# Parts of W_out spread over 46 steps of attention instead of 50, with the heads' parts and turned blocks placed anew, and another order at the boundary to the MLP

## The chip, the cores and the metric

The kernel runs on one core of a Trainium2 chip. The metric is the device time of one execution in microseconds (us), as the median of several runs. A core has five engines that run side by side, each with its own queue of instructions: TensorE (PE, matmuls and transposes), VectorE (DVE), ScalarE (ACT), GpSimd (POOL) and SyncE (SP), whose queue issues the DMAs. They wait for one another through semaphores.

## The reference, cut to what matters

One layer of a trunk with four token mixers side by side, on x of 1024 positions by 1024 columns; then an MLP of width 4096; then a final norm. The mixer that matters here is A, attention with 4 heads and two softmax maps per head.

```python
def _diff_attention(q, k, v, lam, lam_init, subln_g):
    ...
        s = jnp.einsum('bqhmd,bkhmd->bhmqk', q_blk, k,
                       preferred_element_type=jnp.float32) * scale + bias[None, :, None]
        p = jax.nn.softmax(s, axis=-1)
        w = p[:, :, 0] - lam * p[:, :, 1]
        return jnp.einsum('bhqk,bkhe->bqhe', w.astype(v.dtype), v)
...
        y = jnp.concatenate([y_a, y_b, y_c, y_d], axis=-1)
        x = x + y @ w_out[l]
        xn2 = _rmsnorm(x, norm2_g[l])
        x = x + jnp.square(jax.nn.relu(xn2 @ w_up[l])) @ w_down[l]
    return _rmsnorm(x, final_g)
```

## The kernel before

Rows of x (positions) are handled in 8 row blocks of 128, called tb. A product in float32 is made of three matmuls (`mm3`) of values split into a high and a low part; a split is a cast on ACT (L110) and a subtraction on DVE or POOL (L111). The MLP's product with w_up is made of products of sums of blocks, which is why normed rows are added to one another and turned (transposed) in several combinations: B11, B21, B22 and T1 to T4.

**Attention** (`attention`, L737) runs 64 steps x = 4n + kp, four for each of 16 pairs of a head and two query blocks. In a step PE does in turn: the scores of step x + 6, into a "big" bank (DVE takes the maximum, L648, ACT the exponential, L655, and for a step's pair of maps the two are combined on POOL, on ACT and POOL, or on DVE, L673); `turned`, four transposes of the weights into an "sm" bank (taken out by ACT, L688, or DVE, L690); some of the `fillers`; the step's late items; and `apply` of the step before, 8 matmuls into the "av" bank. There are three "sm" banks, two "big" and one "av".

**Fillers** are the 64 parts of W_out for the mixers B, C and D, spread evenly over the first SL steps (`self.fill`), with a DVE add for every second (L801).

**Late items** come from the table `LATE`. `w_out_a(pr)` gives a list for the row blocks 2pr and 2pr + 1: item 0 is `attended` (4 transposes of the heads' result, taken out by ACT, L767, and DVE, L768); items 1 to 4 are `rows(i, j)`, six matmuls and a DVE add (L833) for a half of a row block. After a row block's second half its sum goes out to `xs` and is normed: ACT squares (L210), DVE scales (L128), POOL takes the power (L124), DVE multiplies (L212). Items 5 to 8 of the pairs 0 and 1 are turns, B11 and B21, two each. A turn is four transposes, two from each of the pair's two normed row blocks, taken out by an ACT cast (L110) and DVE (L111). The lists a0, a1, a2 are those of the pairs 0, 1 and 2. The turns of pair 2, and all of pair 3, are left for the boundary.

**The boundary** (`mlp`, L1157) mixes four kinds of work: f1[p] and f2[p], the first and second half of the first product of w_up's pair p, 12 matmuls each; t, pair 2's ten remaining turns, t[0] and t[1] being B22 and t[2] to t[9] T1 to T4; a, pair 3's items, `attended`, four rows, and ten turns that alternate between the "sm" and "av" banks; and loads and sums of w_up's blocks: `up_load(0)` starts two DMAs (L914), `up_sums(0)` makes four sums on DVE (L919 to L922). After t[1] two sums each of L852 and L853 are made.

**What sets the order.** PE's instructions keep the order of the program (`mm` and `tr` ask for it). For the other engines a scheduler sets the order within each queue before the run. A tile name such as T17 is a buffer: a new tile of that name waits until the last reader of the old one is done.

Of the kernel before, what the change touches and what calls it, by code (L numbers as in the profile page):

```python
# [28 lines left out]
LAM_INIT = 0.8 - 0.6 * math.exp(-0.3 * 0)  # L29
HALF = math.sqrt(0.5)  # L30
NVEC = 77
SL = 50
AHEAD = 6


def LATE(a0, a1, a2):

    return {50: a0[:2], 51: a0[2:3], 52: a0[3:4], 53: a0[4:5] + a1[:1], 54: a1[1:2], 55: a1[2:3],
            56: a1[3:4] + a0[5:7], 57: a1[4:5] + a0[7:8], 58: a0[8:], 59: a2[:1], 60: a2[1:2] + a1[5:6],
            61: a2[2:3] + a1[6:7], 62: a2[3:4] + a1[7:8], 63: a2[4:5] + a1[8:]}, a2[5:]  # L40

# [3 lines left out]
class Trunk:  # L47
# [680 lines left out]
    def attention(self):  # L728
        N = 4 * HEADS
        ahead = 6  # L730
        a = {pr: self.w_out_a(pr) for pr in range(4)}
        late, rest = LATE(a[0], a[1], a[2])
        for n in range(N):
            for kp in range(4):
                m, step = divmod(4 * n + kp + ahead, 4)
                if m < N:
                    self.scores(m, step)  # L737
                self.turned(n, kp)
                if n > 0:
                    if kp == 1:  # L740
                        self.heads_out(n - 1)
                    if kp == 2:
                        self.heads_scaled(n - 1)
                x = 4 * n + kp
                if x < SL:
                    self.fill(64 * (x + 1) // SL - 64 * x // SL)
                for f in late.get(x, ()):
                    f()
                if x == 58:
                    self.first_load(0)  # L750
                if x == 60:
                    self.first_weights(0)
                if kp > 0:
                    self.apply(n, kp - 1)
            self.apply(n, 3)
        self.turns2 = rest
        self.tail = a[3]
# [402 lines left out]
    def mlp(self):  # L1160
        self.heads_out(15)
        self.heads_scaled(15)
        self.fill(len(self.fillers))
        a, t = self.tail, self.turns2
        f1, f2 = zip(*(self.first_parts(p) for p in range(AHEAD)))
        run = lambda fs: [f() for f in fs]
        self.first_load(1)
        self.first_weights(1)
        self.first_load(2)
        run([f1[0], t[0], f1[1], a[0], f2[0], t[1], a[1], a[2], f2[1]] + t[2:4] + a[3:5] + [f1[2]] + t[4:6] + [f1[3]]  # L1170
            + t[6:8] + [f2[2]] + t[8:10] + a[5:7] + [f2[3]])
        self.up_load(0)
        run(a[7:9] + [f1[4]] + a[9:11] + [f1[5]] + a[11:13])
        self.up_sums(0)
        self.split_s12(0)
        run([f2[4]] + a[13:] + [f2[5]])
        self.split_s34(0)
        self.split_a22(0)
        self.again(0)
        self.again(1)  # L1180
        self.up_load(1)
        for p in range(DFF // P // 2):
            self.up_pair(p)
        self.down()
# [25 lines left out]
    def run(self):  # L1210
        self.constants()
        self.groups = [6, 3, 4, 7, 5, 0, 1, 2]
        for x in range(2 * TAPS):
            self.at(16 + 5 * x // 8, lambda x=x: self.conv_tap(x // TAPS, x % TAPS))
        self.at(26, self.mixer_d_load, self.mixer_c_load, self.bias_rows, self.lam)
        for g in range(4):
            self.at(43 + g, lambda g=g: self.mixer_d_gate(g))
        for x in range(4):
            self.at(48 + x, lambda x=x: self.mixer_d_out(x // 2, x % 2))
        for q in range(4):  # L1220
            self.at(42 + q, lambda q=q: self.mixer_c_channels(q))
        self.at(47, self.mixer_c_eight)
        for x in range(4):
            self.at(53 + x, lambda x=x: self.mixer_c_positions(x // 2, x % 2))
        self.at(50, self.mixer_b_load)
        for x in range(4):
            self.at(57 + x, lambda x=x: self.mixer_c_out(x // 2, x % 2))
        for q in range(4):
            self.at(56 + q, lambda q=q: self.mixer_b_norm(q))
        for x in range(4):  # L1230
            self.at(60 + x, lambda x=x: self.mixer_b_silu(x % 2, x // 2))
        for x in range(2):
            self.at(62 + x, lambda x=x: self.scores(0, x))

        self.phase_x()
        self.mixer_b_cols()
        self.mixer_d_v()
        self.mixer_c_cols()
        self.qk_cols(0)
        self.qk_cols(1)  # L1240
        self.st, self.ks, self.qt, self.yt = {}, {}, {}, {}
        self.p1 = ["T14", "gain", "X8", "X9", "X10", "X11"]
        self.subln_s = self.t("sublns", [P, 1])
        self.nc.vector.tensor_scalar(self.subln_s, self.subln, 1.0 - LAM_INIT, None, op0=ALU.mult)
        self.v_cols()
        assert not self.side
        self.wring = ["W0", "W1", "W2", "W3", "W6", "W7"]
        self.load_v()
        self.ya = [self.t(("X14", "X15")[i], [P, 4, 256]) for i in range(2)]
        for x in range(4):  # L1250
            self.scores(*divmod(2 + x, 4))
            self.mixer_b_out(x // 2, x % 2)
        self.fillers += self.w_out_bcd()
        self.ua, self.ub, self.us, self.raw, self.sc, self.xo, self.xn1, self.first_raw = ({} for _ in range(8))
        self.attention()
        self.mlp()
# [99 lines left out]
```

## Time and profile before

| What | Value |
|---|---|
| median of 3 runs | 1133.89 us |
| lowest, highest | 1133.78, 1135.02 us |
| profiled execution | 1133.86 us |
| its span in the profile | 1131.7 us |
| its mean granted clock of TensorE | 0.991 of full speed |
| busy: PE, DVE, ACT, POOL | 96%, 65%, 44%, 27% of the span |

The span is the profile's stretch from the first to the last instruction; 2.2 us of the execution lie around it. Attention runs from about 245 to 473 us of the span, the boundary from there to about 526 us, and the rest of the MLP after it. A wait is shown in the rows as the idle time before an instruction with the instruction that released it, as in `[2.35 <-DVE X L111]`. Busy shares are averages over stages that are bound by different things; a stage is read by itself.

### The profile page before, as it was taken

Reading aid. Unit: us, or ns where it says so; the run is one execution under the profiler, and the core shown is the slowest. Engines: PE = TensorE matmul, PEld = TensorE weight load, DVE = VectorE, ACT = ScalarE, POOL = GpSimd, SP = SyncE. Lnnn points to the kernel's source line nnn. Section 1 sums busy time; section 2 is a strip of 40 time slices with the busy share of each in tenths; the row PEclk is TensorE's granted clock in tenths of the full one; section 3 lists DMA queues with packets and bytes.
Section 4 is the critical chain, followed back from the end, with each engine's and each line's share of the span. In section 5 each row is a group of like instructions: output and inputs, shape, how many; then the busy total and the mean of one; then the engine's idle time right before and its main releaser. Section 6 shows DMA issues by size and latency. Waiting matters only on the chain.

```text
span 1131.7 us, 15023 instructions
## 1 busy us (share of the span) xinstructions
PE 1085.0 (96%) x5836; PEld 918.4 (81%) x5836; DVE 736.6 (65%) x928; ACT 500.7 (44%) x787; POOL 310.5 (27%) x256
## 2 busy tenths in 40 slices
PE   4999999989999998999999999999999999999997
PEld 4989887878999997878777888888778888777885
DVE  4549989758777679785454444434785555986665
ACT  5411313275566656464344444545343333333442
POOL 2000000125456572102777454553400000000001
PEclk9999999999999999999999999999999999999999
DMA  7213126674122102266564444445975553224203
GB/s 270 63 41 92 38 67 212 168 222 157 45 66 71 52 1 94 94 219 228 175 207 177 167 140 168 140 152 162 402 267 171 193 191 117 94 94 168 93 19 149
DMA packets 56660, 159.63 MB, mean 141 GB/s; under 512 B 6411, under 2 KB 8715, under 8 KB 56589
## 3 DMA queue, kind: packets, MB, share of 16 engines
q1 hardware_dynamic: 55581, 156.18, 41.5%
q0 software_dynamic: 1008, 2.49, 0.7%
q8 instruction: 46, 0.75, 0.3%
q14 instruction: 25, 0.20, 0.1%
HBM read 110.41 MB, written 49.28 MB: 141 GB/s over the span
## 4 chain that ended last, share of the span: by engine, by line
PE 84%; DVE 7%; ACT 3%; DMA 2%; issue 2%; SPq 0%; POOL 0%; DVEq 0%; POOLq 0%; ACTq 0%
PE big L104 38%; PE sm L104 32%; PE av L104 10%; PE sm L107 3%; DVE W L111 2%; ACT W L110 1%; DVE T L111 1%; DVE c L648 1%; DMA gain<-in_norm_g_dram 1%; PE av L107 1%; DMA stg<-in_w_out_dram 1%; DVE T L212 0%; DVE T L393 0%; ACT T L210 0%; DVE T L1075 0%
## 5 line engine op out<-in xcount | busy, mean ns | idle before, releaser
L104 PE MATMUL big<-X,W 128*128 128x512 f32 x864 | 211.9, 399 | 2.4 <-DVE T L1007 2.4
L110 ACT CAST W<-stg 128x1024 fp32r<-128x1024 f32 (+1 forms) x93 | 92.1, 994 | 247.9 <-PE big L104 152.8
L104 PEld LDWEIGHTS big<-X,W 128*128 128x128 f32 x864 | 162.9, 190 | 42.1 <-DVE T L1007 4.6
L111 DVE TENSOR_TENSOR W<-stg,W 128x1024 fp32r<-128x1024 f32 x78 | 100.0, 1283 | 128.1 <-ACT W L110 128.0
L124 POOL TENSOR_TENSOR c<-c,mhalf 128x1 f32<-128x1 f32 (+3 forms) x46 | 35.8, 778 | 477.3 <-DVE c L128 405.7
L104 PE MATMUL big<-T,W 128*128 128x512 f32 x648 | 158.7, 397 | 1.1 <-DVE T L111 1.1
L104 PEld LDWEIGHTS big<-T,W 128*128 128x128 f32 x648 | 122.2, 189 | 29.8 <-DVE T L111 1.5
L648 DVE TENSOR_REDUCE c<-big 128x1 f32<-128x1024 f32 x64 | 77.7, 1217 | 26.1 <-PE big L104 26.1
L104 PE MATMUL sm<-W,X 128*128 128x256 f32 (+1 forms) x624 | 89.5, 292 | 1.4 <-DVE c L128 0.9
L110 ACT CAST W<-T 128x1024 fp32r<-128x1024 f32 x48 | 50.3, 1049 | 78.4 <-PE big L104 77.9
L104 PEld LDWEIGHTS sm<-W,X 128*128 128x128 f32 x624 | 79.0, 189 | 4.2 <-DVE c L128 1.1
L104 PE MATMUL sm<-W,T 128*128 128x256 f32 x576 | 80.4, 288 | 0.2 <-DVE T L135 0.2
L104 PE MATMUL big<-W,W 128*128 128x512 f32 x336 | 80.0, 393 | 0.4 <-DVE W L111 0.3
L393 DVE SCALAR_TENSOR_TENSOR T<-T,vec,T 128x1024 f32<-128x1024 f32 x60 | 75.8, 1275 | 0.5
L104 PEld LDWEIGHTS big<-W,W 128*128 128x128 f32 x336 | 63.0, 188 | 15.2 <-DVE W L111 1.3
L111 DVE TENSOR_TENSOR W<-T,W 128x1024 fp32r<-128x1024 f32 x48 | 60.8, 1267 | 17.3 <-ACT W L110 16.9
L104 PEld LDWEIGHTS sm<-W,T 128*128 128x128 f32 x576 | 71.3, 189 | 0.5 <-DVE T L135 0.5
L104 PE MATMUL sm<-T,W 128*128 128x512 f32 x264 | 71.3, 394 | 0.1
L104 PE MATMUL sm<-W,W 128*128 128x512 f32 x240 | 63.7, 393 | 2.0 <-DVE W L111 2.0
L104 PE MATMUL av<-X,X 128*128 128x64 f32 x512 | 62.7, 270 | 1.3 <-DVE X L690 1.3
L104 PEld LDWEIGHTS av<-X,X 128*128 128x128 f32 x512 | 61.6, 191 | 1.8 <-DVE X L690 1.4
L104 PE MATMUL sm<-X,W 128*128 128x512 f32 x216 | 61.9, 394 | 0.0
(277 smaller groups left out, 1863.9 us busy)
## 6 DMA issues: line engine op xcount, KB each, us to landing
stg<-gd SPq DMA_DIRECT2D x52, 512.0 KB, 3.3
gd<-T SPq DMA_DIRECT2D x32, 512.0 KB, 4.6
T<-in_w_down_dram SPq DMA_DIRECT2D x24, 512.0 KB, 4.4
stg<-in_w_up_dram SPq DMA_DIRECT2D x17, 512.0 KB, 4.1
T<-in_x_dram SPq DMA_DIRECT2D x16, 512.0 KB, 6.7
stg<-in_w_in_dram SPq DMA_DIRECT2D x16, 512.0 KB, 4.5
T<-in_w_up_dram SPq DMA_DIRECT2D x16, 512.0 KB, 4.1
gd<-X SPq DMA_DIRECT2D x16, 512.0 KB, 2.8
```

Source lines behind the costliest of these rows:

```text
L104: self.tc.keep_in_program_order(self.nc.tensor.matmul(*a, **k))
L107: self.tc.keep_in_program_order(self.nc.tensor.transpose(out, in_, self.ident))
L110: self.pin(self.nc.scalar.copy(hi, src))
L111: self.pin((eng or self.nc.vector).tensor_tensor(lo, src, hi.bitcast(F32), op=ALU.subtract))
L124: self.pin(self.nc.gpsimd.tensor_tensor(out, in_, self.mhalf[:, :w], op=ALU.pow))
L393: nc.vector.scalar_tensor_tensor(self.acc[c], z[:, j:j + S], self.dw_w[c][:, j:j + 1], self.acc[c], op0=ALU.mult, op1=ALU.add)
L648: nc.vector.tensor_reduce(nm, sc, axis=AX.X, op=ALU.max, negate=True)
```

## The change

It does three things. It spreads the 64 parts over the first 46 steps instead of 50. It places the late items anew: those of pair 0 come one to a step from step 46 on, instead of from 50 with gaps; those of pair 1 follow from 52; those of pair 2 stay at their steps from 59. And it changes the order at the boundary: t[1] ahead of f2[0], t[2] and t[3] ahead of f2[1], all ten turns t ahead of f2[2], and `up_load(0)` and `up_sums(0)` ahead of f1[4]. The work is the same: each engine has as many instructions as before.

```diff
-SL = 50
+SL = 46
...
-    return {50: a0[:2], 51: a0[2:3], 52: a0[3:4], 53: a0[4:5] + a1[:1], 54: a1[1:2], 55: a1[2:3],
-            56: a1[3:4] + a0[5:7], 57: a1[4:5] + a0[7:8], 58: a0[8:], 59: a2[:1], 60: a2[1:2] + a1[5:6],
-            61: a2[2:3] + a1[6:7], 62: a2[3:4] + a1[7:8], 63: a2[4:5] + a1[8:]}, a2[5:]
+    return {46: a0[:1], 47: a0[1:2], 48: a0[2:3], 49: a0[3:4], 50: a0[4:5], 51: a0[5:6], 52: a0[6:7] + a1[:1],
+            53: a0[7:8] + a1[1:2], 54: a0[8:] + a1[2:3], 55: a1[3:4], 56: a1[4:5], 57: a1[5:6], 58: a1[6:7],
+            59: a1[7:8] + a2[:1], 60: a1[8:] + a2[1:2], 61: a2[2:3], 62: a2[3:4], 63: a2[4:5]}, a2[5:]
...
-        run([f1[0], t[0], f1[1], a[0], f2[0], t[1], a[1], a[2], f2[1]] + t[2:4] + a[3:5] + [f1[2]] + t[4:6] + [f1[3]]
-            + t[6:8] + [f2[2]] + t[8:10] + a[5:7] + [f2[3]])
+        run([f1[0], t[0], f1[1], a[0], t[1], f2[0], a[1], a[2]] + t[2:4] + [f2[1]] + a[3:5] + t[4:6] + [f1[2]] + t[6:8]
+            + [f1[3]] + t[8:10])
         self.up_load(0)
-        run(a[7:9] + [f1[4]] + a[9:11] + [f1[5]] + a[11:13])
+        run([f2[2]] + a[5:7] + [f2[3]] + a[7:9])
         self.up_sums(0)
+        run([f1[4]] + a[9:11] + [f1[5]] + a[11:13])
         self.split_s12(0)
```

**TensorE around pair 0's last row part.** Of the kernel before, the end of that row part in step 53 (sm_825, six matmuls, its last one here) and what follows, and further down the first turn that reads its norm's output, T18_826, in step 56:

```order
L104 MATMUL sm_825_4472<-W2_693_3883,stg_795_4360 128x512
L107 MATMUL sm_830_4489<-ident_1_63,X14_314_2255 128x128 x4
...
L104 MATMUL sm_857_4592<-W2_693_3883,stg_831_4494 128x512
L107 MATMUL sm_862_4604<-ident_1_63,T17_804_4402 128x128 x2
L107 MATMUL sm_862_4604<-ident_1_63,T18_826_4480 128x128 x2
```

Of the changed kernel, the same row part in step 50 (sm_803) and the turn in step 51 (sm_818), whose second half reads T18_804:

```order
L104 MATMUL sm_803_4396<-W2_670_3807,stg_766_4260 128x512
L104 MATMUL av_796_4374<-X5_313_2252,X12_779_4318 128x64 x4
L104 MATMUL big_808_4417<-X1_586_3430,X6_725_4074 128x512 x2
L104 MATMUL big_808_4417<-diag_5_74,identr_4_72 128x128
L107 MATMUL sm_813_4430<-ident_1_63,X8_743_4163 128x128 x4
L107 MATMUL sm_818_4440<-ident_1_63,T17_781_4328 128x128 x2
L107 MATMUL sm_818_4440<-ident_1_63,T18_804_4404 128x128 x2
L104 MATMUL av_796_4374<-X4_312_2251,X13_802_4393 128x64 x4
```

Three steps lay between the row part and the turn; now an apply (one row of four here), the scores and a turned block do.

**VectorE between the two.** Of the changed kernel, from the reduce of step 50's scores to the eviction of the turn:

```order
L648 TENSOR_REDUCE c1_799_4384<-big_798_4380 128x1
L833 TENSOR_TENSOR T1_379_2460<-sm_803_4396,T1_379_2460 128x512
L690 COPY X13_802_4393<-sm_813_4430 128x512
L128 TENSOR_SCALAR c1_806_4408<-c1_805_4406 128x1
L648 TENSOR_REDUCE c1_809_4421<-big_808_4417 128x1
L212 SCALAR_TENSOR_TENSOR T18_804_4404<-T1_379_2460,c1_807_4410,gain_673_3813 128x1024
L665 RECIPROCAL c1_811_4425<-c4_797_4379 128x1
L667 SCALAR_TENSOR_TENSOR c1_812_4427<-c4_797_4379,neglam_145_925,c1_811_4425 128x1
L673 SCALAR_TENSOR_TENSOR X11_800_4386<-W4_810_4423,c1_812_4427,X11_800_4386 128x1024
L111 TENSOR_TENSOR T6_815_4437<-sm_818_4440,T5_814_4436 128x2x256
```

Of the kernel before, the last of the same chain, T18_826, and the turn's eviction, with another norm between them:

```order
L648 TENSOR_REDUCE c1_841_4535<-big_840_4531 128x1
L690 COPY X13_838_4516<-sm_845_4544 128x512
L212 SCALAR_TENSOR_TENSOR T18_826_4480<-T1_379_2460,c1_829_4486,gain_696_3889 128x1024
L833 TENSOR_TENSOR T2_387_2506<-sm_846_4550,T2_387_2506 128x512
...
L212 SCALAR_TENSOR_TENSOR T19_847_4558<-T2_387_2506,c1_850_4564,gain_696_3889 128x1024
L111 TENSOR_TENSOR T6_859_4601<-sm_862_4604,T5_858_4600 128x2x256
```

The eviction stood eleven rows behind the norm's output; now four.

**VectorE at the boundary.** Of the kernel before, from the first of w_up's sums (T17) to the eviction of the "av" bank (av_992, by a[5]); sm_990 and sm_991 are t[8] and t[9], T13 and stg_996 the two blocks that `up_load(0)` loads:

```order
L919 TENSOR_TENSOR T17_1008_5279<-T13_997_5204 128x512
L921 TENSOR_TENSOR T18_1009_5280<-stg_996_5203,T13_997_5204 128x512
L111 TENSOR_TENSOR W7_984_5142<-W4_954_5012,W6_983_5141 128x1024
L920 TENSOR_TENSOR T17_1008_5279<-T17_1008_5279,stg_996_5203 128x512
L852 TENSOR_TENSOR stg_948_4981<-stg_948_4981,T19_847_4558 128x512
L852 TENSOR_TENSOR stg_963_5048<-stg_963_5048,T20_875_4654 128x512
L111 TENSOR_TENSOR T12_987_5148<-sm_990_5151,T4_986_5147 128x2x256
L111 TENSOR_TENSOR gain_989_5150<-sm_991_5158,W0_988_5149 128x2x256
L111 TENSOR_TENSOR X1_934_4899<-av_992_5165,X0_933_4898 128x2x256
L922 TENSOR_TENSOR T18_1009_5280<-stg_996_5203,T17_1008_5279 128x512
```

Of the changed kernel, the same stretch; t[8] and t[9] are sm_987 and sm_988, a[5] is av_994:

```order
L919 TENSOR_TENSOR T17_1000_5221<-T13_990_5144 128x512
L921 TENSOR_TENSOR T18_1001_5222<-stg_989_5143,T13_990_5144 128x512
L111 TENSOR_TENSOR T12_984_5126<-sm_987_5129,T4_983_5125 128x2x256
L920 TENSOR_TENSOR T17_1000_5221<-T17_1000_5221,stg_989_5143 128x512
L111 TENSOR_TENSOR gain_986_5128<-sm_988_5136,W0_985_5127 128x2x256
L922 TENSOR_TENSOR T18_1001_5222<-stg_989_5143,T17_1000_5221 128x512
L852 TENSOR_TENSOR stg_948_4981<-stg_948_4981,T19_853_4571 128x512
L852 TENSOR_TENSOR stg_963_5048<-stg_963_5048,T20_871_4644 128x512
L111 TENSOR_TENSOR W7_992_5164<-W4_960_5030,W6_991_5163 128x1024
L853 TENSOR_TENSOR T19_853_4571<-T19_853_4571,stg_948_4981 128x512
L111 TENSOR_TENSOR X1_934_4899<-av_994_5169,X0_933_4898 128x2x256
```

The evictions of the turns come sooner in the row, L922 and an L853 now stand ahead of the "av" eviction, and on TensorE f2[2]'s twelve matmuls now lie between t[9] and a[5], where they lay ahead of t[8].

## Rows read from the trace of the kernel before

**Rows 1.** Windows: us from:to, length, busy us (instructions) PE, PEld, DVE, ACT, POOL, clock, DMA, GB/s

```profile
420.00:473.00 53.00, 47.13 (x319) 40.91 (x319) 45.75 (x74) 30.49 (x64) 13.01 (x15) 1.00 0.26 90
473.00:526.00 53.00, 49.86 (x253) 41.20 (x253) 38.83 (x59) 29.28 (x55) 9.02 (x8) 0.97 0.55 193
430.00:450.00 20.00, 17.47 (x115) 15.26 (x113) 19.51 (x32) 13.68 (x30) 5.78 (x7) 1.00 0.35 119
...
270.00:420.00 150.00, 150.00 (x1227) 145.35 (x1226) 111.85 (x173) 90.27 (x191) 86.46 (x64) 1.00 0.16 48
```

**Rows 2.** Timeline at the boundary: start, duration, engine, line, operation, count, [wait <-releaser]

```profile
491.52 1.67 PE L104 MATMUL sm<-W,stg 128*128 128x512 f32 x6 [0.78 <-DVE c L128]
...
503.96 0.69 DVE L919 TENSOR_TENSOR T<-T 128x512 f32<-128x512 f32 x1 [1.26 <-PE sm L107]
...
509.31 0.68 DVE L111 TENSOR_TENSOR X<-av,X 128x512 fp32r<-128x512 f32 x1
...
504.77 3.01 PE L104 MATMUL big<-T,T 128*128 128x512 f32 x12
510.14 0.76 PE L107 MATMUL av<-ident,T 128*128 128x128 f32 x4 [2.35 <-DVE X L111]
...
511.41 4.18 PE L104 MATMUL big<-T,W 128*128 128x512 f32 x12
```

**Rows 3.** Windows, as in the first group, for TensorE's clock after waits

```profile
512.00:514.00 2.00, 2.00 (x6) 1.60 (x5) 2.00 (x3) 0.64 (x2) 0.00 (x0) 0.52 0.99 277
...
190.00:194.00 4.00, 1.39 (x16) 1.24 (x17) 4.00 (x6) 1.70 (x3) 0.00 (x0) 0.88 0.11 26
194.00:200.00 6.00, 6.00 (x23) 4.90 (x22) 6.00 (x11) 0.64 (x2) 0.00 (x0) 0.51 0.63 158
...
448.00:450.00 2.00, 0.77 (x7) 0.49 (x5) 2.00 (x3) 1.66 (x3) 0.38 (x1) 1.00 0.76 246
```

**Rows 4.** Timelines of DVE and of ACT in late attention

```profile
433.45 1.21 DVE L648 TENSOR_REDUCE c<-big 128x1 f32<-128x1024 f32 x1
434.58 0.68 DVE L690 COPY X<-sm 128x512 f32<-128x512 f32 x1
...
435.39 1.11 ACT L655 ACTIVATE W<-big,c 128x1024 f32<-128x1024 f32 x1
```

**Rows 5.** Timeline of PE in late attention

```profile
425.23 0.71 PE L104 MATMUL big<-X,X 112*128 112x512 f32 x2
...
425.84 0.60 PE L107 MATMUL sm<-ident,X 128*128 128x128 f32 x4
426.20 1.63 PE L104 MATMUL sm<-W,stg 128*128 128x512 f32 x6
427.67 1.89 PE L104 MATMUL av<-X,X 128*128 128x64 f32 x16
...
450.63 1.65 PE L104 MATMUL sm<-W,stg 128*128 128x512 f32 x6 [1.87 <-DVE T L111]
```

**Rows 6.** Timeline of two norm chains: the quickest, then the slowest's ends

```profile
462.82 1.67 PE L104 MATMUL sm<-W,stg 128*128 128x512 f32 x6 [0.32 <-DVE T L833]
...
465.44 1.06 ACT L210 ACTIVATE X<-T 128x1024 f32<-128x1024 f32 x1
...
466.63 0.15 DVE L128 TENSOR_SCALAR c<-c 128x1 f32<-128x1 f32 x1 [0.36 <-ACT X L210]
...
467.44 1.28 DVE L212 SCALAR_TENSOR_TENSOR X<-T,c,gain 128x1024 f32<-128x1024 f32 x1 [0.66 <-POOL c L124]
...
432.70 1.64 PE L104 MATMUL sm<-W,stg 128*128 128x512 f32 x6
...
443.27 1.28 DVE L212 SCALAR_TENSOR_TENSOR T<-T,c,gain 128x1024 f32<-128x1024 f32 x1
```

**Rows 7.** SP's timeline, and DMA issues (the last number: us from issue to landing)

```profile
495.78 0.38 SPq L914 DMA_DIRECT2D stg<-in_w_up_dram  x1
...
stg<-in_w_up_dram SPq DMA_DIRECT2D x1, 512.0 KB, 6.6
```

## The prediction, made before the changed kernel ran

> **What bounds the kernel now.** Read the windows first. Over the 53 us from 420 to 473, the last steps of attention, TensorE is busy 47.13 us, so it waits 5.87; over the next 53 us, the boundary to the MLP, it is busy 49.86, so it waits 3.14, at a granted clock of 0.97 [rows 1]. Everything that the change moves lies in or before these two stretches. From 270 to 420 it is busy all the time [rows 1], and from the first w_up pair on its instructions keep their order, so there is nothing to be had there but a shift. The most that the change can give is therefore 5.87 + 3.14 us and whatever the low clock cost. That cost is read at the boundary: 12 matmuls begun at 511.41 took 4.18 us where the same 12 begun at 504.77 took 3.01 [rows 2], and the window from 512 to 514 ran at a clock of 0.52 [rows 3]: 1.17 us more. All together 10.2.
>
> Then see who is short in each stretch. From 430 to 450 VectorE (DVE) is busy 19.51 of 20 us while TensorE (PE) is busy 17.47 [rows 1]: there PE waits for DVE. At the boundary PE's one long wait is 2.35 us before the four transposes at 510.14, released by a DVE eviction of the single "av" bank [rows 2], with DVE at work without a break from 503.96 to there. PE waits in program order, so a wait moves all that follows.
>
> **Prices.** In DVE's timeline an instruction's row runs 0.08 us into the next, so the step from start to start is what it costs: 1.13 for a reduce (433.45 to 434.58) and, by the same 0.08, 0.60 for a 128x512 copy or add [rows 4]; the 1.28 of the norm's last instruction, L212 [rows 6], is 1.20, and the combine on DVE (L673, the same kind of instruction, as wide) is put at 1.20 too. On PE a step's scores are 0.61, its turned block 0.36, six matmuls of a row part 1.47 (425.23, 425.84, 426.20, 427.67), eight matmuls of the apply about 0.85 (half of the 16 at 427.67) [rows 5]. The exponential (L655) is 1.11 [rows 4], with its sum read out about 1.2, as the square (L210, 1.06) is followed by the instruction that needs its sum 1.19 after its start [rows 6].
>
> **Part 1: the turned blocks come right behind the norm that they read.** Before, rows(1,1) of pair 0 stood in step 53 and the turn that reads its normed rows in step 56; now in 50 and 51. For pair 1 it was 57 and 60, now 56 and 57. Between a row part and the turn lies a chain: DVE adds (L833), ScalarE squares (L210), DVE scales (L128), GpSimd takes the power (L124), DVE multiplies (L212). The quickest chain in the trace runs from the row part's end, 464.49, to 468.72: 4.2 us, every engine free for it. The slowest runs from 434.34 (432.70 + 1.64) to 444.55 (443.27 + 1.28): 10.2 us, in the stretch where DVE is full, and nobody waited since the turn came three steps later [rows 6].
>
> Step 51. After the row part PE has an apply (0.85), scores (0.61), a turned block (0.36) and two transposes of the other row block (0.2): 2.0 us, then it must have L212's output. So the wait is at least 4.2 - 2.0 = 2.2 and at most 8.2. In the new order the chain has company: a reduce and an exponential of step 50 stand ahead of L210, and step 51's reduce ahead of L212. From the start of that first reduce: 1.13 + 1.2 + 1.2 (L210 with its read-out) + 0.15 (L128) + 1.13 + 1.2 = 6.0; DVE, still at an L212, starts it about 0.3 before the row part ends. So the chain is 5.75, the wait **3.75**.
>
> Step 57. PE has only scores, turned block and two transposes: 1.2 us. On DVE stand the rest of a reduce (0.8), a combine (1.2), L833 (0.6), then L210 (1.2), L128 (0.15), a reduce (1.13), L212 (1.2): 6.3. The wait is **5.1** (from 4.2 - 1.2 = 3.0 up to 9.0).
>
> Between them, in step 53, the turns' evictions (a cast on ScalarE behind an exponential, then DVE's L111) hold the "sm" banks, and the row part waits for `attended` behind a reduce: by a walk along the new order 1.5 + 1.4 = **2.9**. The trace has one wait of this kind, 1.87 us before a row part, for an L111 [rows 5], so 0 to 4. Step 59 has 0.75, small ones 0.3. Sum 12.8, against 5.87 before: **+6.9**.
>
> A bound from below comes from counting. From step 50's reduce to the L212 that step 57 waits for, DVE has 8 reduces (9.0), 5 L833 and 4 L690 and 4 L111 of 0.6 (7.8), 3 L212 and 3 combines (7.2), a split of weights (1.15), `attended` (0.66) and small ones (1.7): 27.5 us. PE has 22.6 in the same stretch, and DVE starts 1.5 behind: the waits are at least 6.4 even if DVE never stops, so with 1.05 after it attention is at +1.5 or more. If DVE did not trail, 4.9: about +0.
>
> The first 46 steps hold the same 64 parts as the 50 did. They are PE's own work in a stretch where PE never waits [rows 1], and their DVE adds are the ones that leave the late steps; I cost that at nothing. If that cover were gone, it would show as PE waits before 415.
>
> **Part 2: the boundary.** Before, f2[2]'s twelve matmuls stand ahead of t8 and t9, whose transposes are the last readers of a tile that L919 overwrites: L919 starts at 503.96, released by PE's transposes, and the eviction for which PE waits ends 6 us later [rows 2]. Now t8 and t9 stand 2.86 us of matmuls earlier and L919 can start under f2[2]. But the sums also need `up_load`'s second half in "stg": issued at 495.78, landed 6.6 us later at 502.4 [rows 7]. From there DVE has L921, two evictions, L920, L922, two L852, a split (1.13), an L853 and the "av" eviction, 9 x 0.6 + 1.13 = 6.5: 508.9, where PE could go at 507.7 (504.77 + 2.9). The wait of 2.35 becomes 1.2; about 0.5 if the load lands 2 us sooner, 2.5 if first_load(5), which now goes out between the two halves, holds it up by its 512 KB. I take 1.4, with 0.5 at t5 (a bank whose add is late) and 0.4 at a9. The wait of 0.78 ahead of a4, at 491.52 [rows 2], goes, f2[1] now covers it. So 2.3 against 3.14 + 1.17, if the low clock goes with the long wait: **-2.0** (from -3.4 to +0.4, where a wait remains with its low clock). The rest of SP's queue moves within several us of slack and is costed at nothing.
>
> **Part 3: the clock.** PE waits longer than before at steps 51 and 57. After the wait of 2.35 the clock fell to 0.52 for two us [rows 3], its 1.2 GHz level, at a cost of 1.17. After 190 to 194, where PE was busy 1.39 of 4 us, it stood at 0.51 for six us [rows 3], which cost about 2.9. In 448 to 450 PE worked 0.77 of 2 us and stayed at 1.00 [rows 3]. So each of the two new gaps costs 0 to 2.9. I take 0.6 each, **+1.2**: half of the nearest row (1.17), since in these steps DVE sets the pace and a slow matmul partly fills what would be a wait.
>
> The Trainium skill ("TensorE: Matmul & The Clock Gate", section "HAM oscillation — how this bites in real kernels") states that waits between bursts of matmuls throttle the clock again, so that each burst starts at half speed. The row at 512 agrees; this speaks against the change, since it trades one such gap for two, and makes the third rival below.
>
> **Sum.** 6.9 - 2.0 + 1.2 = +6.1 on the profiled execution's 1133.86, which is the runs' median (1133.89) within their scatter: **1140.0 us**.
>
> **Rivals.**
> 1. *Faster.* The new waits only take the place of old ones: PE waits at 51 and 57, DVE packs its work into those gaps, and the waits at 53 and 59 are gone. For it: DVE at 19.51 of 20 us shows that PE waited for the same work before, and one chain ran in 4.2. With 2.2 + 3.0 and little else attention is at -0.7 to 0, and the boundary gives its -3.4: 1130.5. It decides from the point where the waits of 51 and 57 add up to under 6 us and the boundary's long wait is under 0.5. Against it: step 50's exponential and two reduces stand in the chain by order. Chance 0.13.
> 2. *No change.* Attention at the packed bound (+1.5), boundary at -2.0, no fall of the clock: 1133.4. A wait of PE is DVE's chance to catch up, so my walk may count the same lateness twice. Chance 0.21.
> 3. *The clock falls at both gaps for long,* as after 190 to 194: +5.8 in place of +1.2, so +10.7: 1144.6. For it: the gaps of 3.75 and 5.1 are longer than the 2.35 that sufficed. Against: row parts follow each gap at once. Chance 0.16.
> The forecast has 0.50.
>
> **Range and chances.** From 1131.5, which leaves out the first rival, to 1144, which leaves out the upper half of the third: some 0.2 outside. 0.2%, about what a measurement of this kernel tells from no change, is 2.3 us: faster than 1131.6 has 0.13, within it 0.21, slower than 1136.2 the forecast and the third rival, 0.66.
>
> **What would show it.** In the new profile PE should have a wait before transposes (L107, "sm" from a T tile), released by DVE's L212, of about 3.75 and another of about 5.1, some 20 us apart, and one for L111 between them; if either is under 2.5, part 1 is wrong. The wait for the "av" eviction near 508 should be 0.5 to 2.5 and the clock behind it 1.00; if it stays at 2.3 with a low clock, part 2 is wrong. A clock near 0.5 just after the new gaps shows part 3. From the first w_up pair on the trace should be the old one, shifted; if it is not, or if PE waits before 415, the prediction is wrong for a reason that I haven't named.

## The result, and the profile after

The changed kernel took 1140.26 us in the median of 4 runs (1139.84 to 1140.50), the kernel before 1133.84 in 4: a ratio of 1.0065, with a 95% interval from 1.0051 to 1.0079. It is 6.4 us slower; 1140.0 was forecast. The span of the profiled execution grew from 1131.7 to 1138.5 us.

The forecast's two waits are there. TensorE's waits in the changed kernel from 420 to 473 us (engine, tile, line, what it waited for: us in total, times, longest):

```profile
PE sm L107 <- DVE T L212: 9.5, 2, 5.0
PE av L104 <- DVE X L690: 1.3, 1, 1.3
PE sm L104 <- DVE stg L768: 1.1, 1, 1.1
PE sm L107 <- DVE T L111: 0.7, 1, 0.7
```

The window of the changed kernel that holds the end of attention, up to the first f1 matmul, with columns as in [rows 1]:

```profile
415.00:482.00 67.00, 54.44 (x344) 49.16 (x342) 50.10 (x80) 33.62 (x73) 15.14 (x17) 0.90 0.21 71
```

TensorE's timeline of the changed kernel around the waits, columns as in [rows 2]:

```profile
427.02 0.38 PE L107 MATMUL sm<-ident,T 128*128 128x128 f32 x2
431.88 0.69 PE L107 MATMUL sm<-ident,T 128*128 128x128 f32 x2 [4.48 <-DVE T L212]
432.36 3.52 PE L104 MATMUL av<-X,X 128*128 128x64 f32 x16
...
438.88 0.71 PE L104 MATMUL big<-X,X 112*128 112x512 f32 x2
...
440.78 0.66 PE L107 MATMUL sm<-ident,T 128*128 128x128 f32 x4 [0.68 <-DVE T L111]
442.57 1.66 PE L104 MATMUL sm<-W,stg 128*128 128x512 f32 x6 [1.13 <-DVE stg L768]
...
456.11 0.38 PE L107 MATMUL sm<-ident,T 128*128 128x128 f32 x2
461.50 0.69 PE L107 MATMUL sm<-ident,T 128*128 128x128 f32 x2 [5.01 <-DVE T L212]
461.98 1.81 PE L104 MATMUL av<-X,X 128*128 128x64 f32 x8
...
467.31 0.60 PE L107 MATMUL sm<-ident,X 128*128 128x128 f32 x4
```

In each gap TensorE has done the two transposes of the other row block, and then stands still until the norm's last instruction. From 270 to 420 us TensorE is busy all the time, as before, so the parts in the first 46 steps cost no wait. The waits of this end of attention are 67.00 - 54.44 = 12.56 us, where before they were 5.87 [rows 1]. Behind each gap comes something that the forecast had priced low: the 16 matmuls of an apply at 432.36 take 3.52 us, where before they took 1.89 [rows 5]. TensorE's granted clock just behind the two gaps, in windows of the changed kernel:

```profile
432.00:438.50 6.50, 6.50 (x30) 6.31 (x31) 3.70 (x7) 2.11 (x8) 1.11 (x2) 0.50 0.00 1
461.50:466.50 5.00, 5.00 (x27) 5.00 (x28) 2.62 (x5) 1.81 (x4) 0.00 (x0) 0.56 0.45 147
```

That is the lower level, 1.2 GHz, for some 6 and 4 us. And VectorE is busy 3.70 of 6.50 us there: behind the first gap it stands idle for 2.80 us and doesn't set the pace.

At the boundary the changed kernel needs 50.82 us from the first f1 matmul (482.38) to the first w_up pair (533.20); before it was 53.35 (473.02 to 526.37). From there on TensorE's instructions are the same in the two traces, 6.7 to 6.8 us apart.

**Where the 6.8 us of span come from.** I take three anchors in each profile: the last early wait of attention (a scores tile whose wait on the exponential ends at 263.45 before and at 261.44 after), the first f1 matmul, and the first w_up pair.

| stretch | before | after | difference |
|---|---|---|---|
| up to the last early wait | 263.45 | 261.44 | -2.0 |
| from there to the first f1 matmul | 209.57 | 220.94 | +11.4 |
| the boundary | 53.35 | 50.82 | -2.5 |

Up to the first anchor TensorE's instructions are the same in both kernels. They part at three places, mostly by TensorE's clock, which falls in one profile and not in the other, or for a longer time. At 22 to 26 us the changed kernel gains 1.5. At 190 to 200, around a wait in the phase of the mixers, it gains 2.0 (0.7 of it a short wait that only the kernel before has). At 250 it loses 1.2, and from its first instruction on it was 0.3 behind. Windows of the first two places, of the kernel before, then of the changed one:

```profile
22.00:27.00 5.00, 4.26 (x25) 4.26 (x26) 3.44 (x6) 1.92 (x4) 0.55 (x1) 0.66 0.10 39
192.00:200.00 8.00, 6.44 (x24) 5.34 (x25) 8.00 (x14) 1.44 (x3) 0.00 (x0) 0.57 0.53 131
```

```profile
22.00:27.00 5.00, 3.98 (x35) 3.98 (x36) 3.68 (x6) 1.97 (x4) 0.55 (x1) 1.00 0.08 34
192.00:200.00 8.00, 8.00 (x55) 6.70 (x53) 7.59 (x13) 1.22 (x3) 0.00 (x0) 0.79 0.71 177
```

In the nine profiles of this study that anchor lies between 260.80 and 263.95, so single profiles differ by up to 3 us in a place that has nothing to do with the change. Whether the changed kernel is ahead there in all its runs, or was by chance in the profiled one, stays open; by the second and third row alone it would be 8.8 us slower. The table below compares stretches for this reason, and not only medians.

### The profile page after: what moved, and what is told of

Its sections match the earlier page's. It is cut to its first block, busy times and chain, and to the rows that moved or that the text cites. A ratio compares the mean times of both kernels' runs of the same rounds, so it can differ in the third digit from the quotient of the medians.

```text
span 1138.5 us, 15012 instructions
## 1 busy us (share of the span) xinstructions
PE 1086.2 (95%) x5836; PEld 920.8 (81%) x5836; DVE 733.7 (64%) x928; ACT 501.8 (44%) x787; POOL 308.9 (27%) x256
## 4 chain that ended last, share of the span: by engine, by line
PE 82%; DVE 8%; DMA 4%; ACT 3%; issue 2%; SPq 1%; POOL 0%; DVEq 0%; POOLq 0%; ACTq 0%
PE big L104 37%; PE sm L104 31%; PE av L104 10%; PE sm L107 3%; DVE W L111 2%; DVE T L111 1%; DMA T<-in_w_down_dram 1%; DMA stg<-in_w_up_dram 1%; ACT W L110 1%; DVE c L648 1%; DMA gain<-in_norm_g_dram 1%; DVE T L212 1%; DMA stg<-in_w_out_dram 1%; DVE T L1075 0%; ACT T L210 0%
## 5 line engine op out<-in xcount | busy, mean ns | idle before, releaser
L104 PEld LDWEIGHTS av<-X,X 128*128 128x128 f32 x512 | 64.8, 199 | 2.1 <-DVE X L690 1.4
L104 PE MATMUL av<-X,X 128*128 128x64 f32 x512 | 65.2, 277 | 1.3 <-DVE X L690 1.3
```

The source lines that it names most:

```text
L104: self.tc.keep_in_program_order(self.nc.tensor.matmul(*a, **k))
```

## The experiments

The theory after the result: the changed steps cost about 9.5 us of waits for L212 at steps 51 and 57, as forecast, and a low clock behind each; the boundary gives back 2.5. The rivals: VectorE's work is packed into too few steps wherever the turns stand; the low clock costs little; the two parts don't add up.

**The steps alone.** The boundary's order is that of before (also in the lines after the one shown), the rest is the changed kernel.

```diff
-        run([f1[0], t[0], f1[1], a[0], t[1], f2[0], a[1], a[2]] + t[2:4] + [f2[1]] + ...
+        run([f1[0], t[0], f1[1], a[0], f2[0], t[1], a[1], a[2], f2[1]] + t[2:4] + ...
```

> The steps' table and the 46 steps as changed, the boundary's order as before. Theory (attention's waits plus the low clock behind them cost about 9, the boundary gives back about 2.5, and the two add up): the two waits for L212 of 4.5 and 5.0 us stay, the boundary takes again about 53.3 us from the first f1 matmul to the end of f2[5], and the time is 1140.3 + 2.5 = 1142.8. Rival (the boundary's gain comes only because pair 2's late items end otherwise, so it belongs to attention): 1140.3, boundary at 50.8.

Measured: 1143.08 us, ratio 1.0084 (1.0065 to 1.0103) to 1133.69 of before. Attention (anchor to anchor) 220.90, the boundary 53.29: the changed kernel's attention and the old boundary, each within 0.1 us. The two parts add up.

**The boundary alone.** The table and SL = 50 are those of before.

> The boundary's order as changed, attention as before. Theory: attention's waits as before (5.9 from 420 to 473), the boundary 50.8 us instead of 53.35, so 1133.9 - 2.5 = 1131.4. Rival (the new order gives nothing without the shifted attention): 1133.9.

Measured: 1130.06 us, ratio 0.9978 (0.9966 to 0.9990). The boundary takes 51.23 us, so the new order helps without the new steps. Attention took 1.1 us more than before in this profile, and the rows say why: the same wait of 1.30 us for L690 stands in both traces, and only here the clock fell behind it. Windows of this kernel and then of the kernel before:

```profile
443.00:447.00 4.00, 3.79 (x17) 3.50 (x18) 3.69 (x9) 3.17 (x10) 1.25 (x1) 0.61 0.32 123
```

```profile
443.00:447.00 4.00, 3.59 (x24) 3.20 (x25) 3.93 (x10) 3.36 (x10) 1.29 (x1) 1.00 0.26 103
```

**The turns three steps behind their norm.** The changed kernel with another table:

```diff
-    ... 51: a0[5:6], 52: a0[6:7] + a1[:1], 53: a0[7:8] + a1[1:2], 54: a0[8:] + a1[2:3], 55: a1[3:4], 56: a1[4:5],
-        57: a1[5:6], 58: a1[6:7], 59: a1[7:8] + a2[:1], 60: a1[8:] + a2[1:2], ...
+    ... 52: a1[:1], 53: a1[1:2] + a0[5:6], 54: a1[2:3] + a0[6:7], 55: a1[3:4] + a0[7:8], 56: a1[4:5] + a0[8:],
+        59: a2[:1] + a1[5:6], 60: a2[1:2] + a1[6:7], 61: a2[2:3] + a1[7:8], 62: a2[3:4] + a1[8:], ...
```

> The changed kernel with the turns of pair 0 from step 53 on instead of 51 and those of pair 1 from 59 instead of 57, three steps behind the norm that they read; rows as in the changed kernel but for pair 1, one step later at most. Theory (the cost is the chain from a row part to the turn right behind it, and the low clock that follows its gap): no wait for L212, no clock near 0.5 after 420, attention within 1 us of before, boundary as changed: 1131 to 1132.5. Rival (the cost is DVE's work packed into steps 46 to 57, wherever the turns stand): the waits move to evictions and row parts and stay at 10 us or more: 1137 to 1140.

Measured: 1128.80 us, ratio 0.9961 (0.9946 to 0.9976): 4.9 us faster than before, and some 11 faster than the changed kernel, with the same 46 steps, the same rows and the same work for VectorE. Its attention takes 209.04 us, its waits from 415 to 473 are 4.07 us. What is left of the wait for L212, and the longest one, in TensorE's timeline of this kernel:

```profile
434.99 0.74 PE L104 MATMUL big<-X,X 112*128 112x512 f32 x2 [1.92 <-ACT W L655]
...
457.89 0.44 PE L107 MATMUL sm<-ident,T 128*128 128x128 f32 x2 [0.35 <-DVE T L212]
```

So packing is not the cause; it is the turn's place right behind its norm. This is also the fastest kernel measured here. But most of its gain is the boundary's, which alone gave 3.6: the other 1.3 lies within the two intervals, which overlap, so it isn't shown that 46 steps gain anything over 50. And the profiled execution is the slowest of its 8, 1131.35.

One part of the expectation was missed: the clock did fall, behind the wait of 1.92.

```profile
435.00:438.50 3.50, 3.50 (x12) 3.01 (x13) 3.46 (x5) 2.08 (x3) 0.40 (x1) 0.59 0.00 0
```

The kernel with the sums on GpSimd, further down, has the same attention and the same wait of 1.92, and there the clock stays at 1.00. From that wait's end to the turn behind the next row part the one needs 4.04 us (434.99 to 439.03) and the other 2.46 (432.13 to 434.59), so 1.6; but by the end of attention they differ by only 0.6. Here VectorE is full (3.46 of 3.50 us), and 1.0 of what the low clock costs comes back in the steps behind it.

**Both gaps filled.** In steps 51 and 57 TensorE gets work inside the gap, and nothing else changes:

```diff
                 for k in range(2):
                     o = c + (2 * q + k) * P
                     self.tr(pv[:, k, i * P:(i + 1) * P], x[:, o:o + P])
+                if name == "B11" and q == 0 and i == 0:
+                    for _ in range(36):
+                        self.tr(pv[:, 0, P:2 * P], x[:, c:c + P])
```

> The changed kernel with 36 more transposes of a block that is already there, written to a place that is overwritten next, ahead of the two transposes that wait for L212 in steps 51 and 57: about 3.6 us of TensorE work at 0.1 us each inside each of the two gaps, so that TensorE is not idle there. Theory (the gaps cost twice, by their length and by the half clock behind them, about 3.2 and 2.2 us): the clock stays at 1.00, the waits shrink to 1 to 1.5 us, L212 is where it was, and the time falls by about 5.4 to 1135. Rival (the half clock costs nothing since DVE sets the pace there, as the prediction half assumed with 0.6 a gap): 1139 to 1140.3. A third way (transposes do not hold the clock up): the clock falls all the same, 1140.3.

Measured: 1132.65 us, ratio 0.9993 (0.9981 to 1.0005). 72 transposes whose output is overwritten make the kernel 7.6 us faster. TensorE's timeline of this kernel, then the windows behind the gaps:

```profile
427.26 4.31 PE L107 MATMUL sm<-ident,T 128*128 128x128 f32 x38
432.12 0.44 PE L107 MATMUL sm<-ident,T 128*128 128x128 f32 x2 [0.55 <-DVE T L212]
432.40 1.90 PE L104 MATMUL av<-X,X 128*128 128x64 f32 x16
...
435.95 0.72 PE L104 MATMUL big<-X,X 112*128 112x512 f32 x2
...
453.19 4.88 PE L107 MATMUL sm<-ident,T 128*128 128x128 f32 x40
457.91 1.00 PE L104 MATMUL av<-X,X 128*128 128x64 f32 x8
...
461.35 0.60 PE L107 MATMUL sm<-ident,X 128*128 128x128 f32 x4
```

```profile
432.00:438.00 6.00, 5.70 (x44) 5.04 (x44) 5.24 (x10) 4.29 (x14) 1.10 (x2) 1.00 0.00 1
458.00:463.00 5.00, 5.00 (x49) 5.00 (x47) 4.17 (x7) 2.83 (x5) 0.00 (x0) 1.00 0.37 122
```

So the third way in the expectation falls, and so does the rival. L212 comes no sooner in step 51 (432.1 against 431.9), but the clock is 1.00 behind both gaps. That prices the low clock: from 431.88 to the scores at 438.88 the changed kernel needs 7.00 us, this one from 432.12 to 435.95 only 3.83, so 3.2; from the apply at 461.98 to the turned block at 467.31 it needs 5.33, this one from 457.91 to 461.35 only 3.44, so 1.9. Together 5.1 of the 7.6. The rest: the second gap is about 1.2 us shorter, and the wait of 1.26 for L690 at 470 is gone. That VectorE and ScalarE get their inputs sooner once TensorE runs at full clock would explain both, but isn't shown.

**The first gap filled alone.** The same lines, with `and pr == 0`.

> The changed kernel with the 36 additional transposes in step 51 alone. Theory (each gap has its own low clock, whose cost adds up): the clock stays at 1.00 after the first gap and falls to 0.5 for 4 to 5 us after the second as in the changed kernel; of the 7.6 that filling both gave, about 3.2 and the small waits of step 53: 1136 to 1137. Rival (the two falls are one thing: with the first gone the second gap starts from another state and does not lower the clock): 1133.

Measured: 1134.43 us, ratio 1.0014 (1.0003 to 1.0025) to 1132.58 of before on the same chip, so 1.9 above it where 2.3 to 3.3 was expected, and where both gaps filled gave -1.0. The low clock is still there behind the second gap, at 0.55, as TensorE's timeline and a window of this kernel show:

```profile
458.40 0.69 PE L107 MATMUL sm<-ident,T 128*128 128x128 f32 x2 [4.07 <-DVE T L212]
```

```profile
458.00:464.00 6.00, 5.60 (x30) 5.60 (x31) 3.31 (x6) 2.25 (x6) 0.00 (x0) 0.55 0.39 142
```

Each gap brings its own fall; the second doesn't hang on the first. The second gap is a microsecond shorter all the same, as it is with both filled: with the first fall gone, the second gap shrinks too, and the wait for L690 at 470 is gone here as well.

**The turns one step later.** Pair 0's from 52, pair 1's from 58.

```diff
+    ... 52: a0[5:6] + a1[:1], 53: a0[6:7] + a1[1:2], 54: a0[7:8] + a1[2:3], 55: a0[8:] + a1[3:4], 56: a1[4:5],
+        58: a1[5:6], 59: a1[6:7] + a2[:1], 60: a1[7:8] + a2[1:2], 61: a1[8:] + a2[2:3], ...
```

> The changed kernel with pair 0's turns from step 52 and pair 1's from step 58, one step later than there, two steps behind the norm. Theory (wait = chain - TensorE's work between): pair 0 gets 2.0 + 1.7 + 1.0 = 4.7 us of work against a chain of 6.5 as measured (2.0 + 4.5), so a wait of about 1.8 and no low clock; pair 1 gets 1.2 + 1.2 = 2.4 against 6.2, so a wait of about 3.8 with a low clock behind it for some 4 us: attention gives back 2.7 + 3.2 for the first gap and 1.2 for the second, 7 of the 7.6 come only if the second gap shrinks below what lowers the clock: 1133 to 1135. Rival (once turns are not next to the norm, a step more gives nothing further): as with the turns three steps behind, 1129.

Measured: 1137.67 us, ratio 1.0038 (1.0025 to 1.0051) to 1132.58. That is 5.1 above before where -0.7 to +1.3 was expected: a miss. The waits for L212 came as expected, 1.33 and 4.01, and only behind the second the clock is low. TensorE's timeline of this kernel, then two windows:

```profile
434.46 0.44 PE L107 MATMUL sm<-ident,T 128*128 128x128 f32 x2 [1.33 <-DVE T L212]
438.07 0.66 PE L107 MATMUL sm<-ident,T 128*128 128x128 f32 x4 [1.78 <-DVE T L111]
439.86 1.65 PE L104 MATMUL sm<-W,stg 128*128 128x512 f32 x6 [1.13 <-DVE stg L768]
...
459.55 0.69 PE L107 MATMUL sm<-ident,T 128*128 128x128 f32 x2 [4.01 <-DVE T L212]
```

```profile
434.00:440.00 6.00, 2.63 (x18) 2.07 (x19) 5.76 (x10) 5.19 (x9) 1.10 (x2) 1.00 0.02 8
459.00:465.00 6.00, 5.46 (x27) 5.46 (x27) 4.14 (x7) 1.71 (x4) 0.00 (x0) 0.50 0.36 100
```

What I left out is the wait that the shorter gap uncovers: step 53 now waits 1.78 + 1.13 for evictions, from 434 to 440 VectorE is busy 5.76 of 6 us. By stretches attention is 215.07, so 5.9 less than in the changed kernel, close to the 7 that I had put there; but this profile's first anchor lies at 263.95, 2.5 later than the changed kernel's, and that takes part of it from the medians.

**The first pair's sums on GpSimd,** on top of the turns three steps behind.

```diff
-        tt = (self.nc.gpsimd if p else self.nc.vector).tensor_tensor
+        tt = self.nc.gpsimd.tensor_tensor
```

> The kernel with turns three steps behind, and the four sums of the first w_up pair (L919 to L922) on GpSimd instead of VectorE. Theory (TensorE's wait of 2.2 us at the boundary is VectorE's queue, four sums of 0.6 us and a load that the second of them waits for): VectorE reaches the av eviction 2.4 us sooner, the wait goes or falls under 0.5 and the time by about 2 us against the kernel with turns three steps behind: 1126.7. Rival (GpSimd's sums, 1.3 us each where VectorE needs 0.6, come late for the splits that follow, or slow VectorE meanwhile): a wait at a later eviction takes its place, 1128.5 to 1130.

Measured: 1130.42 us, ratio 0.9982 (0.9971 to 0.9994) to 1132.58: 2.2 below before, where the same kernel with the sums on VectorE was 4.9 below. Its boundary takes 52.87 us where that one's takes 51.28. Timelines of this kernel, GpSimd and VectorE, then TensorE:

```profile
499.82 1.29 POOL L920 TENSOR_TENSOR T<-T,stg 128x512 f32<-128x512 f32 x1
500.38 2.99 DVE L852 TENSOR_TENSOR stg<-stg,T 128x512 f32<-128x512 f32 x2 [1.86 <-PE sm L107]
501.19 1.62 POOL L922 TENSOR_TENSOR T<-stg,T 128x512 f32<-128x512 f32 x1
...
505.03 0.68 DVE L111 TENSOR_TENSOR X<-av,X 128x512 fp32r<-128x512 f32 x1
...
505.85 0.76 PE L107 MATMUL av<-ident,T 128*128 128x128 f32 x4 [2.51 <-DVE X L111]
...
507.12 4.19 PE L104 MATMUL big<-T,W 128*128 128x512 f32 x12
```

VectorE's timeline of the kernel with turns three steps behind, the same two L852:

```profile
505.24 1.28 DVE L852 TENSOR_TENSOR stg<-stg,T 128x512 f32<-128x512 f32 x2
```

The wait didn't go: 2.51 where that kernel had 2.21. The theory was half right. Without the sums VectorE does come sooner: L852 starts 0.07 us after f2[3]'s first matmul (500.31), there 1.47 after it (503.77). Sooner it can't, since L852 overwrites a tile that a[6]'s transposes read. But the two L852, with GpSimd's sums beside them, take 2.99 us instead of 1.28, and that uses up the 1.4 gained. With 1.28 here the wait would be about 0.8, by my estimate from these rows. That GpSimd slows VectorE meanwhile was part of the rival; its 1128.5 to 1130 was too low too.

| kernel | median | before there | attention, anchor to anchor | boundary |
|---|---|---|---|---|
| before | 1133.84 | | 209.57 | 53.35 |
| changed | 1140.26 | 1133.84 | 220.94 | 50.82 |
| steps alone | 1143.08 | 1133.69 | 220.90 | 53.29 |
| boundary alone | 1130.06 | 1133.69 | 210.71 | 51.23 |
| turns three steps behind | 1128.80 | 1133.69 | 209.04 | 51.28 |
| both gaps filled | 1132.65 | 1133.69 | 213.56 | 50.39 |
| turns one step later | 1137.67 | 1132.58 | 215.07 | 50.81 |
| first gap filled | 1134.43 | 1132.58 | 215.64 | 50.41 |
| sums on GpSimd | 1130.42 | 1132.58 | 208.43 | 52.87 |

The last two columns are of the one profiled execution, which isn't always near the median: it was the slowest of 8 with the turns three steps behind, the second slowest of 10 with the boundary alone (1132.43), and the fastest of 5 with the turns one step later (1136.90).

## Why the prediction was right, point by point

**Step 51 and step 57 (part 1).** Forecast 3.75 and 5.1, measured 4.48 and 5.01. The chain is made as it was added up. VectorE's timeline of the changed kernel around step 51:

```profile
425.81 1.22 DVE L648 TENSOR_REDUCE c<-big 128x1 f32<-128x1024 f32 x1
426.95 0.68 DVE L833 TENSOR_TENSOR T<-sm,T 128x512 f32<-128x512 f32 x1
427.55 0.68 DVE L690 COPY X<-sm 128x512 f32<-128x512 f32 x1
429.35 0.15 DVE L128 TENSOR_SCALAR c<-c 128x1 f32<-128x1 f32 x1 [1.12 <-ACT T L210]
429.42 1.22 DVE L648 TENSOR_REDUCE c<-big 128x1 f32<-128x1024 f32 x1
430.55 1.28 DVE L212 SCALAR_TENSOR_TENSOR T<-T,c,gain 128x1024 f32<-128x1024 f32 x1
```

From the first reduce's start, 425.81, to L212's end, 431.83, it is 6.02 us, where 6.0 was added up, with the second reduce between L128 and L212. The row part had ended at 425.32 (423.69 + 1.63), 0.5 before that reduce began, where the forecast had it end 0.3 after: this is the 0.7 by which the wait was longer.

**Step 53.** Forecast 1.5 + 1.4, measured 0.68 + 1.13: too much by 1.1. Why stays open. The low clock ahead of it isn't the reason: from the scores behind the first gap to the second gap's first transposes the changed kernel needs 17.23 us (438.88 to 456.11), and with both gaps filled, at a clock of 1.00, it is 17.24 (435.95 to 453.19). Step 59's place was taken by a wait of 1.26 (forecast 0.75). The sum of waits was 12.8 by forecast and is 12.56.

**The clock (part 3): the step that failed.** Forecast +1.2, measured +5.1 (3.2 + 1.9, by the kernel with both gaps filled). The price of one gap was taken as half of the row at the boundary, since "in these steps DVE sets the pace and a slow matmul partly fills what would be a wait". The windows behind the gaps show the opposite: VectorE, busy 3.70 of 6.50 and 2.62 of 5.00 us, stood idle for much of the time beside a slow TensorE. The third rival had priced the two falls at 5.8, close to what came.

The Trainium skill ("TensorE: Matmul & The Clock Gate", section "HAM oscillation — how this bites in real kernels"), with its rule that a wait between bursts lowers the clock, agrees with both gaps here: 0.50 and 0.56 behind them.

**The boundary (part 2).** Forecast -2.0, measured -2.5. The rows of the changed kernel, VectorE and then TensorE:

```profile
511.46 0.69 DVE L921 TENSOR_TENSOR T<-stg,T 128x512 f32<-128x512 f32 x1 [0.66 <-DMA stg<-in_w_up_dram]
...
517.42 0.68 DVE L111 TENSOR_TENSOR X<-av,X 128x512 fp32r<-128x512 f32 x1
...
518.24 0.63 PE L107 MATMUL av<-ident,T 128*128 128x128 f32 x4 [1.79 <-DVE X L111]
...
519.06 3.05 PE L104 MATMUL big<-T,W 128*128 128x512 f32 x12
```

The load in "stg" does hold L921, and 6.6 us of VectorE lie from there to the eviction's end (6.5 forecast). The wait is 1.79 (1.4 forecast), the 12 matmuls behind it take 3.05 instead of 4.18 [rows 2], and the wait ahead of the fourth row part is gone. All waits of the boundary come to 2.1 where 2.3 was forecast, the small ones to 0.3 instead of 0.9. TensorE's busy time fell from 50.21 to 48.75, by 1.46 where 1.17 was forecast. These two make the difference. The kernel with the sums on GpSimd shows that the load is only one of two limits: there L852 waits for a[6].

**The sum.** 6.1 was forecast and 6.4 measured, but part of that is luck. By stretches the terms are +6.7 (waits; 6.9 forecast), +5.1 (clock; 1.2), -2.5 (boundary; -2.0), which is +9.3 against +8.8 in the table, and -2.0 in a stretch ahead of them that the forecast had at nothing. The clock's term was 3.9 too low. The stretch ahead takes back 2.0 of it, the waits and the boundary 0.7, and 0.5 is in no term. So the mechanism of the waits and of the boundary held, and the total is near only because an error in the clock's term met a difference in a place that the change doesn't touch.

**The rivals.** That the new waits only take the place of old ones falls: the old waits, 1.87 and 1.30, went or stayed, and 9.5 came on top. That they come to the bound of a packed VectorE falls too: it was busy only 50.10 of the 67 us. The third rival's mechanism is the one that came: the clock fell behind both gaps, for 5.1 where it had 5.8. Its time, 1144.6, didn't come, for the reasons under the sum.

## What to carry to other kernels

When work is moved sooner, look at what it reads: an engine in program order stands still for the whole chain (here 6 us through five instructions on three engines), and three steps of distance hid it where one or two didn't. A long gap on TensorE can have a second price behind it, the low clock. Another engine that was full before the gap need not hide it: behind the first gap here VectorE was busy 3.70 of 6.50 us. Two profiles are compared by stretches between the same instructions, since a place that has nothing to do with a change can differ by 2 to 3 us.

## What the runs showed of the hardware that I had not expected

Transposes held the clock up. In the kernel with both gaps filled TensorE did nothing but 128x128 transposes against the identity for 4.3 and 4.9 us, and the clock stood at 1.00 behind them. The Trainium skill ("TensorE: Matmul & The Clock Gate", section "Part 4: PE-mode transpose") states that the full clock doesn't engage for transpose mode, which doesn't count as TensorE being busy "the same way". For these float32 transposes the measurement says otherwise; whether they run in that mode isn't shown by the rows.

The same wait can have both outcomes. Behind waits of 1.79 (changed kernel) and 2.21 us (turns three steps behind) at the boundary the 12 matmuls took 3.05, behind 2.35 (before), 2.36 (steps alone) and 2.51 (sums on GpSimd) 4.18, 4.60 and 4.19. But the wait of 1.30 in attention was followed by a clock of 0.61 in one profile and of 1.00 in another, and the wait of 1.92 by 0.59 and by 1.00. What the chip does in between isn't shown by these rows, so the second price of such a wait is a chance, not a number. All six waits of 4.0 to 5.0 us for L212, in four kernels, had a low clock behind them.

Two of VectorE's adds of 128x512 tiles took 1.28 us together with GpSimd idle and 2.99 while GpSimd added tiles of the same size. Of GpSimd's own the one wholly beside them (L922) took 1.62, where the one that was done before they began (L921) took 1.30.
